# Tail of a hybrid encoder block on one core: order of the last branch blocks, tile pools of the output projection, and the place of loads on the DMA queue

## The chip, the core and the metric

The kernel runs on one core of a Trainium2 chip. A core has five engines with instruction streams of their own: TensorE (PE, matmuls; weight loads are listed apart as PEld), VectorE (DVE), ScalarE (ACT), GpSimd (POOL) and SyncE (SP), which here only issues DMA transfers. Each engine works its stream off in order, and an instruction that waits for a semaphore holds up everything behind it on its engine. SP's stream is the DMA queue of nearly all loads; POOL issues the stores to scratch tensors in device memory and a few loads. The metric is the device time of one execution in microseconds (us), as the median of several runs.

## The reference, cut to what matters

All arrays are float32, with 1024 tokens and width 1024, one layer.

```python
h = rmsnorm(x, norm_g) * (1 + scale) + shift
p = h @ w_in          # q, k, v, z_gla, decay ranks, u, vs, z_gmlp, m_gla, m_gmlp
o = gla(q, k, v, decay)            # both directions, 4 heads, chunks of 64
o = o * rsqrt(mean(o * o) + EPS) * gla_norm_g
y_gla  = (o * silu(z_gla)) @ w_br_gla
y_gmlp = (gelu(u) * spatial_gate(vs) * silu(z_gmlp)) @ w_br_gmlp
merged = sigmoid(m_gla) * y_gla + sigmoid(m_gmlp) * y_gmlp
out = rmsnorm(x + gate * (merged @ w_out), final_g)
```

What follows concerns the last fifth of the kernel: the end of the attention of the last head, the product with `w_br_gmlp` (called yb), the product with `w_br_gla` (ya), the merge, and the product with `w_out` (the projection, o).

## The kernel before, in words

Every float32 operand of a large product is split into a high part (a cast, `S.copy` on ACT to the reduced float32r format) and a low part (the difference, on DVE); each product is three matmuls, high by high, high by low and low by high. `split_w` (L172 to L174) does a split, `stage` (L165) loads 512 KB of weights into a staging tile by a DMA on SP, `fm_weights` (L179) stages and splits the weights of one block of 128 output features, and `tm_weights` (L196) does so for four pieces of a 512-column half of `w_out`, with an optional step on the staged piece in between; for `w_out` that step is `scale_cols` (L1197), which multiplies it by the gate on POOL (L1199).

The program is traced in Python and then ordered by a planner. For each engine it takes the earliest instruction in program order whose inputs, by a timing model, are ready, and lays the streams out that way before the run; tiles are given out in the same pass. `tc.issue_after(ins)` puts what its block traces on the engine of `ins` behind `ins`. Tiles come from pools with a fixed number of buffers: "h" (30 of 128x1024, `ht`), "w" (13 of 128x1024, `w4`), "s" (18 of 128x512, `w2`), and PSUM accumulators "d" (3, `pd`). A DMA into a tile waits until the buffer's last user is done.

**The attention and its filler.** `order` lists 16 units (head, direction and half of the tokens). Between their parts, `dense(n)` (called with `QUOTA`) takes steps of a generator, `filler()` (L1056), which runs a list of jobs: q, k and v products of later heads and then the yb blocks. A job is a pair: what fetches its weights, and what runs it in steps of 12 matmuls (`fm_half`, L965). `filler` fetches the next job's weights after the first step of the job before. yb blocks 0 and 1 run as two jobs, a half of the tokens each, for both blocks (`run_two`); blocks 2 to 7 are one job each, first half, then second half. The evacuation `ev_yb` (L987) loads `tb`, multiplies, and stores to `y2_d`. The input of yb is `GG`, sixteen "h" tiles (high and low of four pieces for each half of the tokens).

`key_ops` (L836) transposes the keys of a unit and casts them (`keh`, L843). The output of a unit is normalised, gated with `z_t` (`zg`) and stored to `g_d`.

**ya.** `GO`, again sixteen "h" tiles, is the gated attention output: for three of four pieces it is loaded back from `g_d` into `gf` (L1126) and split, for the last head it is split from `z_t`. `ya_steps` (L1159, matmuls L1165 to L1167) runs blocks of 128 features: blocks 0 to 2 interleaved, then blocks 3 to 7 one after the other, each with the first half of the tokens and then the second, 24 matmuls a half. `ev_ya` (L1134) loads `ta` and `y2` of its block and half (L1145, L1146), merges on DVE (L1147, L1148) and splits the result into `M` (cast L1149, difference L1150).

**Projection.** `w_o` holds the two 512-column halves of `w_out` (`tm_weights`, L196); the first in "w" tiles, the second in "h" tiles. `dense_o` runs 24 matmuls (`tm_step`, L209 to L211) for each of eight blocks of 128 tokens, with the first three ahead up to their last step. `ev_first` (L1202) loads the residual `res` (L1204, in "h" tiles), adds the accumulator, and multiplies by the final gain `fg` on POOL; `ev_last` adds the second half, normalises and stores.

Of the kernel before, what the change touches and what calls it, by code (L numbers as in the profile page):

```python
# [9 lines left out]
F32 = mybir.dt.float32  # L10
# [7 lines left out]
P = 128  # L18
D = 1024
T = 1024  # L20
KC = D // P
# [10 lines left out]
FB_Q, FB_K, FB_Z, FB_U, FB_ZG, FB_MA, FB_MB, FB_YA, FB_YB = 0, 4, 8, 16, 24, 32, 40, 48, 56  # L32


WVS, WV, WO = 0, 8, 14
# [5 lines left out]
PR_FG, PR_BG, PR_BS, PR_C = 0, 1, 2, 3  # L41
# [3 lines left out]
def hybrid_block_kernel(ctx: ExitStack, tc: tile.TileContext, x, wf, wt, wada, wgate, wvr, wst, alpha, abias,  # L45
                        pcols, prows, out):
    nc = tc.nc
    V, S, G, TE = nc.vector, nc.scalar, nc.gpsimd, nc.tensor
# [20 lines left out]
    y2_d = dram("y2_d", [KC, P, T])  # L69
# [3 lines left out]
    ta_d = dram("ta_d", [KC, P, T])  # L73
# [44 lines left out]
    def ht(shape, dtype, name):  # L118
        return hp.tile(shape, dtype, tag="h", bufs=30, name=nm(name))

    def w4(shape, dtype, name):
        return hp.tile(shape, dtype, tag="w", bufs=13, name=nm(name))
# [38 lines left out]
            H.make(c, half)  # L161

    pin = [True]

    def stage(src):  # L165
        w = w4([P, 1024], F32, "ws")
        i = nc.sync.dma_start(w, src)
        if pin[0]:
            tc.keep_in_program_order(i)
        return w  # L170

    def split_w(w, hi, lo):  # L172
        S.copy(hi, w)  # L173
        V.tensor_tensor(out=lo, in0=w, in1=hi.bitcast(F32), op=ALU.subtract)  # L174

    def flat(t):
        return t.rearrange("p k c -> p (k c)")

    def fm_weights(b):  # L179
        w = stage(wf[b])  # L180
        hi, lo = w4([P, KC, P], F32R, "wh"), w4([P, KC, P], F32R, "wl")
        split_w(w, flat(hi), flat(lo))
        return hi, lo
# [12 lines left out]
    def tm_weights(w0, new, prep=None):  # L196
        pieces = []
        for j in range(4):
            w = stage(wt[w0 + j])
            if prep is not None:  # L200
                prep(w)
            hi, lo = new[j]([P, 2, 512], F32R, "th"), new[j]([P, 2, 512], F32R, "tl")
            split_w(w, flat(hi), flat(lo))
            pieces.append((hi, lo))
        return pieces
# [32 lines left out]
    for b in range(2):  # L238
        pc = pd()
        sl = slice(b * 512, b * 512 + 512)  # L240
# [162 lines left out]
    for a, e in ((0, 3), (3, 6), (6, 8)):  # L403
        n = (e - a) * NV0
        w = w4([P, 1024], F32, "ws")
        nc.sync.dma_start(w[:, 0:n], wvr[:, a * NV0:e * NV0])
        new = w4 if e == KC else ht
        hi, lo = new([P, e - a, NV0], F32R, "tvh"), new([P, e - a, NV0], F32R, "tvl")
# [44 lines left out]
    for b in range(2):  # L453
        pw = pm()
        TE.matmul(pw, lhsT=ones, rhs=wsT[:, 4 * b:4 * b + 4, :].rearrange("p g t -> p (g t)"), start=True, stop=True)
        for i in range(4):
            g = 4 * b + i
# [267 lines left out]
    for c in range(2):  # L725
        hi, lo = H.make(c, 1)
# [109 lines left out]
    def key_ops(un):  # L836
        kh = un["kh"]
        pt = pm()
        for i in range(4):
            TE.transpose(pt[:, i * P:(i + 1) * P], kh[:, i * P:(i + 1) * P], ident)  # L840
        keh = w2([P, 512], F32R, "keh")
        kel = w2([P, 512], F32R, "kel")
        S.copy(keh, pt)  # L843
        V.tensor_tensor(out=kel, in0=pt, in1=keh.bitcast(F32), op=ALU.subtract)
        un.update(keh=keh, kel=kel)

# [25 lines left out]
    units = {}  # L872
# [80 lines left out]
    GG = Act("gg")  # L953
# [33 lines left out]
    def ev_yb(j):  # L987
        def ev(half, acc):
            sl = slice(half * 512, half * 512 + 512)
            t = w2([P, 512], F32, "tb")  # L990
            nc.sync.dma_start(t, tb_d[j, :, sl])
            V.scalar_tensor_tensor(out=t, in0=t, scalar=1.0, in1=acc, op0=ALU.add, op1=ALU.mult)
            G.dma_start(y2_d[j, :, sl], t)
        return ev
# [20 lines left out]
    def run_two(x, evacs):  # L1015

        def run(half):
            def f(ws):
                for w, ev in zip(ws, evacs):
                    yield from fm_half(x, w, half, ev)  # L1020
            return f
        return run
# [3 lines left out]
    held = {}  # L1026

    def hold(name, f):
        def g():
            held[name] = f()  # L1030
            return held[name]
        return g
# [5 lines left out]
    def gg_second():  # L1038
# [3 lines left out]
    jobs = [(lambda: prep_qk(0, True), run_fm(H, ev_k(0))),  # L1042
            (lambda: prep_qk(1, False), run_fm(H, ev_q(1))),
            (lambda: prep_qk(1, True), run_fm(H, ev_k(1))),
            (lambda: v_weights(2, w4), run_v(2)),
            (lambda: prep_qk(2, False), run_fm(H, ev_q(2))),
            (lambda: prep_qk(2, True), run_fm(H, ev_k(2))),
            (lambda: v_weights(3, w4), run_v(3)),
            (hold("qk3", lambda: [prep_qk(3, False), prep_qk(3, True)]), qk3(1)),
            (lambda: held["qk3"], qk3(0)),  # L1050
            (hold("yb", gg_first), yb0(0)),
            (gg_second, yb0(1))]
    for j in range(2, KC):
        jobs.append((lambda j=j: fm_weights(FB_YB + j), run_fm(GG, ev_yb(j), (0, 1))))

    def filler():  # L1056
        ready = jobs[0][0]()
        for n, (_, run) in enumerate(jobs):
            now = ready
            first = True  # L1060
            for _ in run(now):
                if first and n + 1 < len(jobs):
                    ready = jobs[n + 1][0]()
                first = False
                yield

    fill = filler()
# [51 lines left out]
    for half in range(2):  # L1119
        for c in range(KC // 2):  # L1120
            hi, lo = GO.make(c, half)
            sl = slice(half * 512, half * 512 + 512)
            if c < 3:
                g = ht([P, 2, 512], F32, "gf")
                for i in range(2):
                    nc.sync.dma_start(g[:, i, :], g_d[2 * c + i, :, sl])  # L1126
                split_w(flat(g), flat(hi), flat(lo))
            else:
                for i in range(2):
                    split_w(z_t[HEADS - 1][i][:, sl], hi[:, i, :], lo[:, i, :])  # L1130
# [3 lines left out]
    def ev_ya(j, half, acc):  # L1134
        if j < KC - 1:
            if half == 0:
                for n in "hl":
                    M[j, n] = ht([P, T], F32R, "m" + n)
            mh, ml = (M[j, n][:, half * 512:half * 512 + 512] for n in "hl")
        else:  # L1140
            mh, ml = (w2([P, 512], F32R, "m" + n) for n in "hl")
        M[j, half] = mh, ml
        sl = slice(half * 512, half * 512 + 512)
        y2, m = w2([P, 512], F32, "y2"), w2([P, 512], F32, "ta")
        nc.sync.dma_start(m, ta_d[j, :, sl])  # L1145
        nc.sync.dma_start(y2, y2_d[j, :, sl])  # L1146
        V.scalar_tensor_tensor(out=m, in0=m, scalar=1.0, in1=acc, op0=ALU.add, op1=ALU.mult)  # L1147
        V.tensor_tensor(out=m, in0=m, in1=y2, op=ALU.add)  # L1148
        S.copy(mh, m)  # L1149
        V.tensor_tensor(out=ml, in0=m, in1=mh.bitcast(F32), op=ALU.subtract)  # L1150
# [4 lines left out]
        return mh[:, o], ml[:, o]  # L1155

    ya_w, ya_acc = {}, {}

    def ya_steps(j, half, k0, k1):  # L1159
        if k0 == 0:  # L1160
            ya_acc[j, half] = pd()
        acc = ya_acc[j, half]
        hi, lo = ya_w[j]
        for k in range(k0, k1):
            TE.matmul(acc, lhsT=hi[:, k, :], rhs=GO.hi(k, half), start=(k == 0), stop=False)  # L1165
            TE.matmul(acc, lhsT=lo[:, k, :], rhs=GO.hi(k, half), start=False, stop=False)  # L1166
            TE.matmul(acc, lhsT=hi[:, k, :], rhs=GO.lo(k, half), start=False, stop=(k == KC - 1))  # L1167


    for j in range(3):  # L1170
        ya_w[j] = fm_weights(FB_YA + j)
        ya_steps(j, 0, 0, 6)
    for j in range(3):
        ya_steps(j, 0, 6, KC)
        ev_ya(j, 0, ya_acc[j, 0])
    for j in range(3):
        ya_steps(j, 1, 0, KC)
        ev_ya(j, 1, ya_acc[j, 1])
    for j in range(3, KC):
        ya_w[j] = fm_weights(FB_YA + j)  # L1180
        for half in range(2):
            ya_steps(j, half, 0, KC)
            ev_ya(j, half, ya_acc[j, half])


    fg = w4([P, D], F32, "fg")
    G.dma_start(fg, prows[PR_FG].partition_broadcast(P))

    res = [None] * NT
    ev_o = []  # L1190
# [6 lines left out]
    def scale_cols(w, b):  # L1197
        w3 = w.rearrange("p (k c) -> p k c", k=2)
        G.tensor_tensor(out=w3, in0=w3, in1=gate[b].unsqueeze(1).broadcast_to([P, 2, 512]),  # L1199
                        op=ALU.mult)  # L1200

    def ev_first(t, acc):  # L1202
        res[t] = ht([P, D], F32, "res")
        nc.sync.dma_start(res[t], x[t * P:(t + 1) * P, :])  # L1204
        r0 = res[t][:, 0:512]
        ev_o.append(V.tensor_tensor(out=r0, in0=acc, in1=r0, op=ALU.add))
        jk = w2([P, 512], F32, "jk")
        s0 = tiny([P, 1], "o_s0", 2)
        S.activation(jk, r0, AF.Square, accum_out=s0)
        ms[t] = tiny([P, 1], "o_ms", 8)  # L1210
        V.tensor_scalar(ms[t], s0, 1.0 / D, EPS, op0=ALU.mult, op1=ALU.add)
        G.tensor_tensor(out=r0, in0=r0, in1=fg[:, 0:512], op=ALU.mult)
# [39 lines left out]
            o_steps(t, KC - 1 if t in ahead else 0, KC)  # L1252
            evac(t, accs[t])

    w_o = [tm_weights(WO, [w4] * 4, lambda w: scale_cols(w, 0))]
    dense_o(w_o[0], ev_first, range(NT), range(3))
    with tc.issue_after(ev_o[2].ins):
        w_o.append(tm_weights(WO + 4, [ht] * 4, lambda w: scale_cols(w, 1)))
# [79 lines left out]
```

## Time and profile before

| | us |
|---|---|
| median of 3 runs | 1096.53 (1094.05 to 1097.13) |
| the profiled execution | 1096.96 |
| its span | 1095.3 |
| mean granted clock of TensorE | 0.988 of full |
| PE busy, 850 to 900 | 44.22 of 50 |
| PE busy, 950 to 1000 | 38.65 of 50 |
| PE busy, 1000 to 1050 | 50.00 of 50 |
| granted clock, 950 to 1000 | 0.91 |

The profile is one execution, seen by the hardware. "Busy" counts the time in which an engine had an instruction at work; matmuls are pipelined, so a row may show 0.39 us for a matmul while the next starts 0.23 later. "Span" runs from the first to the last instruction; the device time has a little around it. In a row of the timeline stand the start, the length, the engine, the line, the operation and its tiles, how many instructions the row merges, and in brackets the idle time ahead of it and what ended it. In the list of waits stand engine, tile and line, what was waited for, and then the total, the count and the longest. SPq is the queue of SP.

### The profile page before, as it was taken

Reading aid. Unit: us, or ns where it says so; the run is one execution under the profiler, and the core shown is the slowest. Engines: PE = TensorE matmul, PEld = TensorE weight load, DVE = VectorE, ACT = ScalarE, POOL = GpSimd, SP = SyncE. Lnnn points to the kernel's source line nnn. Section 1 sums busy time; section 2 is a strip of 40 time slices with the busy share of each in tenths; the row PEclk is TensorE's granted clock in tenths of the full one; section 3 lists DMA queues with packets and bytes.
Section 4 is the critical chain, followed back from the end, with each engine's and each line's share of the span. In section 5 each row is a group of like instructions: output and inputs, shape, how many; then the busy total and the mean of one; then the engine's idle time right before and its main releaser. Section 6 shows DMA issues by size and latency. Waiting matters only on the chain.

```text
span 1095.3 us, 14011 instructions
## 1 busy us (share of the span) xinstructions
PE 1057.6 (97%) x5292; PEld 892.7 (82%) x5292; DVE 641.1 (59%) x960; ACT 412.1 (38%) x721; POOL 276.1 (25%) x304
## 2 busy tenths in 40 slices
PE   6899999999999999999999999999999989995997
PEld 4688899888888888878888898998888778884886
DVE  5777497346547464664554576658767556345522
ACT  4454334233333323343323546457254253111322
POOL 2311203424334352453402001102011010005510
PEclk9899999999999999999999999999999999997999
DMA  9532276233233323223348024347344385235012
GB/s 362 215 128 70 104 253 221 79 118 104 106 116 106 125 97 119 103 104 135 135 145 291 17 83 149 131 140 250 128 161 136 127 294 183 83 119 193 1 58 96
DMA packets 57032, 152.80 MB, mean 140 GB/s; under 512 B 7457, under 2 KB 15649, under 8 KB 56966
## 3 DMA queue, kind: packets, MB, share of 16 engines
q1 hardware_dynamic: 42198, 102.42, 27.0%
q0 software_dynamic: 14768, 49.50, 12.5%
q8 instruction: 41, 0.67, 0.3%
q14 instruction: 25, 0.20, 0.1%
HBM read 108.90 MB, written 43.00 MB: 139 GB/s over the span
## 4 chain that ended last, share of the span: by engine, by line
PE 81%; DVE 5%; issue 5%; DMA 4%; ACT 2%; POOL 1%; SPq 0%; POOLq 0%; ACTq 0%; DVEq 0%
PE pd L210 5%; PE pd L211 5%; PE po L589 4%; PE po L587 4%; PE po L588 4%; PE pd L209 4%; PE pd L969 4%; PE pd L970 4%; PE pd L971 4%; PE pk L587 3%; PE pk L589 3%; PE pk L588 3%; PE pd L587 3%; PE pd L588 3%; PE pd L589 3%
## 5 line engine op out<-in xcount | busy, mean ns | idle before, releaser
L543 PE MATMUL pd<-tvh,hh 128*128 128x256 f32 (+1 forms) x256 | 75.0, 293 | 0.0
L544 PE MATMUL pd<-tvl,hh 128*128 128x256 f32 (+1 forms) x256 | 73.8, 288 | 0.0
L545 PE MATMUL pd<-tvh,hl 128*128 128x256 f32 (+1 forms) x256 | 73.4, 287 | 0.0
L219 POOL TENSOR_TENSOR r<-ms,nhalf 128x1 f32<-128x1 f32 (+1 forms) x24 | 21.6, 900 | 193.1 <-DVE ms L218 184.5
L589 PE MATMUL pd<-hh,al 128*128 128x512 f32 x160 | 62.5, 390 | 0.0
L587 PE MATMUL pd<-hh,ah 128*128 128x512 f32 x160 | 62.3, 390 | 0.0
L588 PE MATMUL pd<-hl,ah 128*128 128x512 f32 x160 | 62.3, 389 | 0.0
L209 PE MATMUL pd<-th,mh 128*128 128x512 f32 x120 | 47.0, 403 | 7.8 <-ACT th L173 7.8
L969 PE MATMUL pd<-ggh,wh 128*128 128x512 f32 x128 | 51.8, 405 | 1.8 <-ACT wh L173 1.8
L210 PE MATMUL pd<-tl,mh 128*128 128x512 f32 x120 | 48.3, 403 | 3.5 <-DVE tl L174 3.5
L971 PE MATMUL pd<-ggh,wl 128*128 128x512 f32 x128 | 51.6, 405 | 0.0
L970 PE MATMUL pd<-ggl,wh 128*128 128x512 f32 x128 | 51.1, 399 | 0.0
L174 DVE TENSOR_TENSOR al<-wa,ah 128x1024 fp32r<-128x1024 f32 x20 | 31.4, 1571 | 32.7 <-PE po L588 30.8
L1167 PE MATMUL pd<-gl,wh 128*128 128x512 f32 x128 | 49.8, 389 | 0.0
L1166 PE MATMUL pd<-gh,wl 128*128 128x512 f32 x128 | 49.6, 389 | 0.0
L1165 PE MATMUL pd<-gh,wh 128*128 128x512 f32 x128 | 49.6, 389 | 0.0
L610 POOL TENSOR_TENSOR wsum<-wb 128x512 f32<-128x512 f32 x20 | 25.8, 1288 | 94.2 <-DMA wb<-in_wf 69.7
L544 PEld LDWEIGHTS pd<-tvl,hh 128*128 128x128 f32 x256 | 48.7, 190 | 0.9 <-issue 0.5
L543 PEld LDWEIGHTS pd<-tvh,hh 128*128 128x128 f32 x256 | 48.7, 190 | 0.8 <-issue 0.5
L545 PEld LDWEIGHTS pd<-tvh,hl 128*128 128x128 f32 x256 | 48.7, 190 | 0.0
L211 PE MATMUL pd<-th,ml 128*128 128x512 f32 x120 | 48.0, 400 | 0.0
L174 DVE TENSOR_TENSOR wl<-ws,wh 128x1024 fp32r<-128x1024 f32 x24 | 29.3, 1220 | 30.0 <-ACT wh L173 28.8
(318 smaller groups left out, 3108.0 us busy)
## 6 DMA issues: line engine op xcount, KB each, us to landing
ws<-in_wf SPq DMA_DIRECT2D x24, 512.0 KB, 5.3
ws<-in_wt SPq DMA_DIRECT2D x22, 512.0 KB, 4.8
wa<-in_wf SPq DMA_DIRECT2D x20, 512.0 KB, 3.6
wb<-in_wf SPq DMA_DIRECT2D x20, 512.0 KB, 4.6
wa<-in_wada SPq DMA_DIRECT2D x16, 512.0 KB, 9.3
xn<-in_x SPq DMA_DIRECT2D x8, 512.0 KB, 7.4
sg_d<-sg POOLq DMA_DIRECT2D x16, 256.0 KB, 3.1
wg<-in_wgate SPq DMA_DIRECT2D x16, 256.0 KB, 5.3
```

Of the source, the lines that this page charges most:

```text
L209: TE.matmul(acc, lhsT=xh, rhs=hi[:, k % 2, :], start=(k == 0), stop=False)
L210: TE.matmul(acc, lhsT=xh, rhs=lo[:, k % 2, :], start=False, stop=False)
L211: return TE.matmul(acc, lhsT=xl, rhs=hi[:, k % 2, :], start=False, stop=(k == KC - 1))
L543: TE.matmul(acc, lhsT=H.hi_t(k, t), rhs=hi, start=(k == 0), stop=False)
L544: TE.matmul(acc, lhsT=H.hi_t(k, t), rhs=lo, start=False, stop=False)
L545: i = TE.matmul(acc, lhsT=H.lo_t(k, t), rhs=hi, start=False, stop=(k == KC - 1))
L587: TE.matmul(acc, lhsT=a, rhs=xh(k), start=(first and k == 0), stop=False, skip_group_check=not first)
L588: TE.matmul(acc, lhsT=a, rhs=xl(k), start=False, stop=False, skip_group_check=not first)
L589: TE.matmul(acc, lhsT=b, rhs=xh(k), start=False, stop=(k == 3), skip_group_check=not first)
L969: TE.matmul(acc, lhsT=hi, rhs=x.hi(k, half), start=(k == 0), stop=False)
L970: TE.matmul(acc, lhsT=hi, rhs=x.lo(k, half), start=False, stop=False)
L971: TE.matmul(acc, lhsT=lo, rhs=x.hi(k, half), start=False, stop=(k == KC - 1))
```

## The change

yb blocks 6 and 7 become two jobs as blocks 0 and 1 are: both blocks for the first half of the tokens, then both for the second. The filler may fetch two jobs ahead: for the last four jobs the third step also fetches. The splits of `gf` are put behind the cast of the last unit's keys on ACT. ya's block 3 is fetched before the second round of blocks 0 to 2, and each later block a block earlier than it is run; blocks 5 to 7 run the first half of the tokens for all three and then the second. The loads of `ta` and `y2` go behind the latest staged weights on SP, and the loads of the residual behind the last `y2`. `res` moves from "h" to "w" tiles, and the first half of `w_out` from "w" to "h" tiles. The final gain is loaded after the weights' first half is traced.

```diff
     def stage(src):
         w = w4([P, 1024], F32, "ws")
         i = nc.sync.dma_start(w, src)
+        last_w[0] = i
...
-        S.copy(keh, pt)
+        un["ins"] = S.copy(keh, pt)
...
-    for j in range(2, KC):
+    for j in range(2, KC - 2):
         jobs.append((lambda j=j: fm_weights(FB_YB + j), run_fm(GG, ev_yb(j), (0, 1))))
 
+    yb6 = run_two(GG, [ev_yb(j) for j in range(KC - 2, KC)])
+    jobs.append((hold("yb6", lambda: [fm_weights(FB_YB + j) for j in range(KC - 2, KC)]), yb6(0)))
+    jobs.append((lambda: held["yb6"], yb6(1)))
+
     def filler():
-        ready = jobs[0][0]()
+        ready = [jobs[0][0]()]
         for n, (_, run) in enumerate(jobs):
-            now = ready
-            first = True
-            for _ in run(now):
-                if first and n + 1 < len(jobs):
-                    ready = jobs[n + 1][0]()
-                first = False
+            now = ready.pop(0)
+            for part, _ in enumerate(run(now)):
+
+                if part == 0 or part == 2 and n >= len(jobs) - 4:
+                    want = n + 2 + part // 2
+                    for m in range(n + 1 + len(ready), min(want, len(jobs))):
+                        ready.append(jobs[m][0]())
                 yield
...
-                split_w(flat(g), flat(hi), flat(lo))
+                with tc.issue_after(units[order[-1]]["ins"].ins):
+                    split_w(flat(g), flat(hi), flat(lo))
...
-        nc.sync.dma_start(m, ta_d[j, :, sl])
-        nc.sync.dma_start(y2, y2_d[j, :, sl])
+
+        with tc.issue_after(last_w[0].ins):
+            nc.sync.dma_start(m, ta_d[j, :, sl])
+            last_y2[0] = nc.sync.dma_start(y2, y2_d[j, :, sl])
...
+    ya_w[3] = fm_weights(FB_YA + 3)
     for j in range(3):
         ya_steps(j, 0, 6, KC)
         ev_ya(j, 0, ya_acc[j, 0])
     for j in range(3):
         ya_steps(j, 1, 0, KC)
         ev_ya(j, 1, ya_acc[j, 1])
-    for j in range(3, KC):
-        ya_w[j] = fm_weights(FB_YA + j)
+    for j in range(3, 5):
+        ya_w[j + 1] = fm_weights(FB_YA + j + 1)
         for half in range(2):
             ya_steps(j, half, 0, KC)
             ev_ya(j, half, ya_acc[j, half])
 
-
-    fg = w4([P, D], F32, "fg")
-    G.dma_start(fg, prows[PR_FG].partition_broadcast(P))
+    for half in range(2):
+        for j in range(5, KC):
+            if half == 0 and j + 1 < KC:
+                ya_w[j + 1] = fm_weights(FB_YA + j + 1)
+            ya_steps(j, half, 0, KC)
+            ev_ya(j, half, ya_acc[j, half])
+
...
-        res[t] = ht([P, D], F32, "res")
-        nc.sync.dma_start(res[t], x[t * P:(t + 1) * P, :])
+        res[t] = w4([P, D], F32, "res")
+        with tc.issue_after(last_y2[0].ins):
+            nc.sync.dma_start(res[t], x[t * P:(t + 1) * P, :])
...
-    w_o = [tm_weights(WO, [w4] * 4, lambda w: scale_cols(w, 0))]
+    w_o = [tm_weights(WO, [ht] * 4, lambda w: scale_cols(w, 0))]
+    fg = w4([P, D], F32, "fg")
+    G.dma_start(fg, prows[PR_FG].partition_broadcast(P))
     dense_o(w_o[0], ev_first, range(NT), range(3))
```

More of the change, by code (lines that the diff above doesn't have):

```diff
@@ L163, in hybrid_block_kernel @@
     pin = [True]
+    last_w = [None]
     def stage(src):
@@ L1157, in hybrid_block_kernel @@
     ya_w, ya_acc = {}, {}
+    last_y2 = [None]
     def ya_steps(j, half, k0, k1):
```

## The prediction

> **What bounds the kernel now.** I read the page first: which engine is full, and where it is not.
>
> ```profile
> span 1095.3 us, 14011 instructions
> PE 1057.6 (97%) x5292; PEld 892.7 (82%) x5292; DVE 641.1 (59%) x960; ACT 412.1 (38%) x721; POOL 276.1 (25%) x304
> PE   6899999999999999999999999999999989995997
> ```
>
> PE is the bound, and the change neither adds nor removes a matmul. So the time can fall only where PE stands still or runs at a reduced clock. After the start the row of 40 slices is at 9 but for an 8 (slice 33, the last unit of the attention), a 5 (slice 37, the step from the last branch product, ya, L1165, to the output projection, L209) and the end. The waits of PE from 800 us on name them all, and the stage table shows that nothing is to be had between them.
>
> ```profile
> PE pd L209 <- ACT th L173: 7.8, 1, 7.8
> PE pd L210 <- DVE tl L174: 3.5, 1, 3.5
> PE pm L830 <- DVE b L821: 2.6, 1, 2.6
> PE pd L969 <- ACT wh L173: 1.8, 1, 1.8
> PE po L848 <- DVE zg L948: 0.7, 1, 0.7
> PE po L946 <- ACT op L937: 0.5, 1, 0.5
> ...
> 900.00:950.00 50.00, 50.00 (x222) 41.39 (x222) 26.37 (x36) 11.80 (x15) 1.09 (x2) 1.00 0.47 158
> ```
>
> **Step 1, the large gap.** PE's timeline, with start, length and waits, the first three lines from the end of the attention for the pace:
>
> ```profile
> 885.74 0.50 PE L969 MATMUL pd<-ggh,wh 128*128 128x512 f32 x1 [1.83 <-ACT wh L173]
> ...
> 886.31 0.39 PE L969 MATMUL pd<-ggh,wh 128*128 128x512 f32 x1
> 886.54 0.40 PE L970 MATMUL pd<-ggl,wh 128*128 128x512 f32 x1
> ...
> 985.50 0.39 PE L1167 MATMUL pd<-gl,wh 128*128 128x512 f32 x1
> 993.72 1.65 PE L209 MATMUL pd<-th,mh 128*128 128x512 f32 x3 [7.83 <-ACT th L173]
> 998.89 0.80 PE L210 MATMUL pd<-tl,mh 128*128 128x512 f32 x1 [3.52 <-DVE tl L174]
> 999.48 0.63 PE L211 MATMUL pd<-th,ml 128*128 128x512 f32 x1
> ...
> 1004.18 0.51 PE L209 MATMUL pd<-th,mh 128*128 128x512 f32 x1
> 1004.52 0.40 PE L210 MATMUL pd<-tl,mh 128*128 128x512 f32 x1
> ```
>
> At full pace two such matmuls start 0.23 us apart (886.31, 886.54; 0.227 over longer stretches); after the gap they start 0.43 apart (12 of them from 999.48 to 1004.18). From 985.50 to 1004.52 are 19.02 us, in which 17 matmuls start (1, 3, 1 and the 12); at 0.227 they need 3.86. The gap costs **15.2 us**: the waits of 11.3 and 3.9 of cold clock. Its cause stands on SP's queue:
>
> ```profile
> SPq L1204 <- PE pd L1167: 43.7, 4, 41.7
> ...
> 976.18 4.99 SPq L1204 DMA_DIRECT2D res<-in_x  x8
> 981.25 0.51 SPq L1145 DMA_DIRECT2D ta<-ta_d  x1
> ...
> 983.46 23.49 SPq L167 DMA_DIRECT2D ws<-in_wt  x7
> ```
>
> The first residual load stands for 41.7 us at the head of SP's queue, until a ya matmul frees its "h" tile. Behind it are the last merge pair and seven of the eight projection weights. They come at 981 and 983, after eight residual loads, and the first casts and the POOL scalings follow only at 992.6. The change takes this apart in three ways. The residual goes to "w" tiles and behind the last y2 load. Projection halves hi and lo go to "h" tiles, so staging needs 4 "w" tiles and not 12. And the order of blocks 5 to 7 (three first halves, then three second halves) frees the eight first-half tiles of GO while 3 x 24 matmuls x 0.227 = 16.3 us of ya are still to run. In those 16.3 us must happen four casts, four subtractions, and ahead of them the four POOL scalings (the groups by tile, with least, median and longest ns; the landing is that of the staged weights):
>
> ```profile
> L1199 POOL TENSOR_TENSOR ws<-ws,gate x4: 2361/2604/3344, 958.8 to 997.7; 128x1024 f32<-128x1024 f32 x4
> L173 ACT CAST th<-ws x3: 1040/1045/1045, 992.6 to 997.8; 128x1024 fp32r<-128x1024 f32 x3
> L174 DVE TENSOR_TENSOR tl<-ws,th x2: 3360/3370/3380, 995.5 to 998.8; 128x1024 fp32r<-128x1024 f32 x2
> DMA to landing us min/median/max: 3.5/5.9/9.1
> ```
>
> Even one after the other at their worst rows the subtractions take 4 x 3.38 = 13.5, after a cast of 1.04: 14.6, still inside 16.3. The scalings need only staging tiles and the gate rows; the first ran at 958.8 before, 27 us ahead of ya's end, and held nothing up. Three blocks' weights hold 6 of 13 "w" tiles, four staged pieces and the final gain 5: eleven, so they fit. I take the whole 15.2 as gone. What is late next is the first residual, due when three projection tokens have run, 72 matmuls x 0.227 = 16 us after ya; the eight loads took 4.99 us to issue, and a load of the same 512 KB lands in 5.9, at most 9.1. No cost.
>
> **Step 2, the end of the attention.** Two places. The first:
>
> ```profile
> 853.45 0.28 PE L850 MATMUL pk<-vh,kel 128*128 128x256 f32 x1
> 856.33 1.16 PE L830 MATMUL pm<-qh,b 128*128 128x128 f32 x8 [2.60 <-DVE b L821]
> 857.24 0.48 PE L969 MATMUL pd<-ggh,wh 128*128 128x512 f32 x1
> ...
> 861.20 0.39 PE L970 MATMUL pd<-ggl,wh 128*128 128x512 f32 x1
> ...
> 756.85 0.89 PE pm L830 x8
> ```
>
> From 853.45 to 861.20 are 7.75 us; the work in them at full pace is 0.12 for the L850, 0.89 for the eight L830 (the last line, a group that waits for nothing) and ten 512-column matmuls, 2.27: **4.5 us** lost. The chain of work leads back to a load:
>
> ```profile
> 842.50 4.42 DMA gf<-g_d
> ...
> 854.46 1.21 DVE gl L174
> ```
>
> ACT's own timeline, around it and later:
>
> ```profile
> 846.95 1.05 ACT L173 CAST gh<-gf 128x1024 fp32r<-128x1024 f32 x1 [1.32 <-DMA gf<-g_d]
> ...
> 865.14 0.59 ACT L843 CAST keh<-pm 128x512 fp32r<-128x512 f32 x1 [4.33 <-PE pm L840]
> 869.80 0.37 ACT L930 COPY op<-po 128x256 f32<-128x256 f32 x1 [4.07 <-PE po L929]
> ```
>
> ACT stands in order: the cast of GO's third tile waits for its load, and the decay chain (e, L796) waits behind it. The idle time ahead of that cast is 1.32; with its 1.05 that is 2.4, and the subtraction of 1.21 on DVE sits in the same chain: 3.6 us against a wait of 2.6. The change puts the six casts behind the cast of the last unit's keys (865.1), so the chain is free of them. I take 4.5 as gone. The second place is the last unit itself, where fillers are short:
>
> ```profile
> 877.44 7.18 DMA ws<-in_wf
> ```
>
> The weights of yb block 7 are issued at 877.44, because SP's queue holds merge loads ahead of them that wait for "s" tiles and stores. PE waits 1.8 for them, and 0.7 and 0.5 more in steps with nothing to put between. The change fetches blocks 6 and 7 together in the second half of block 4, and holds the merge loads back until ya's fourth weight is issued. That is 20 us and more ahead of the use, against 5.9 to land. These **3.0 us** go too, and since the trace before shows no slow matmuls behind them, nothing more.
>
> [...] The wait of 1.8 was followed by full pace, that of 2.6 by slow matmuls up to 861.20, those of 7.8 and 3.5 by twelve. [...]
>
> **What is added.** The held-back casts: three (3 x 1.05 on ACT, 3 x 1.21 on DVE) now fall in 865 to 873, where ACT idled 4.07 us at a stretch, but where DVE also forms the running state (L867) that PE waits for. At worst each holds a state up by its length: 3.6 us; at best 0, since yb fillers now are there. I take one of three, 1.2. The weights' loads now stand ahead of the merge loads, which landed thus:
>
> ```profile
> DMA to landing us min/median/max: 3.0/3.6/9.3
> ```
>
> The first merge pair is needed 13.6 us after ya begins (60 matmuls), ya's fourth weight is issued by its beginning at the latest, and 5.9 for the weight and 3.6 for a pair fit. I take 0 to 4 for a wait at ya's new order, and 1.5 of it, nearest to the waits of 0.5 to 1.8 that the trace has at such joints. Below nothing none of this can go: in 900 to 950 PE is busy 50.00 of 50 at clock 1.00. Fetching block 5 to 7 by halves adds no instruction.
>
> **Sum.** 15.2 + 4.5 + 3.0 = 22.7 out, 2.7 in: 20.0. The profiled run took 1096.96 for a span of 1095.3, so 1.66 lie around it; its time less 20.0 is 1077.0. The median shown, 1096.53, lies 0.4 below that run. Forecast **1077**; the floor is 1096.96 - 22.7 = 1074.3, and with that 0.4 and the spread of the runs shown (1094.05 to 1097.13) down to 1072.5.
>
> **Rivals.**
> A, only the large gap goes (15.2), and the attention's waits stay or are replaced by others of like size: 1096.96 - 15.2 = 1081.8, with 1 to 2 around it. For it: the order of ACT and DVE there is the planner's, made from estimated times, and before it also put a cast ahead of a late load.
>
> B, the scalings and the merge meet. One merge sum (L1148) that ran beside the first scaling took 2.35 us, the others 0.69:
>
> ```profile
> L1148 DVE TENSOR_TENSOR ta<-ta,y x16: 681/692/2350, 915.4 to 991.4; 128x512 f32<-128x512 f32 x16
> ```
>
> Now all four scalings run beside merges: 4 x 1.66 = 6.6 on the path if it decides, so 1077 + 6.6 = 1083.6; with cold clock after it up to 1086. Against it: with three accumulators each merge has the 24 matmuls of the next half, 5.4 us, as cover. [...]
>
> C, the wait returns under another name: the planner puts a load that waits for a tile ahead of the weights again, and the gap stays: 1094 to 1097.
>
> D, slower: SP's order becomes a chain. Every merge load now stands behind a weight load that waits for a "w" tile. If staged projection weights, the gain and early residuals hold nine or more of 13 tiles, a block's weights can be loaded only when the block before gives up its tiles: 5.9 landing, 1.05 cast, 1.21 subtraction, 8.2 us for each of blocks 3 to 7, 41 in all, less the 22.7: about 1115. It decides from nine tiles on; by my count of program order they hold five until block 7 is staged, since residuals come last.
>
> **How the numbers follow.** Forecast (1073 to 1080) 0.58; A 0.19; B 0.11; C 0.05; D 0.07. The range 1072.5 to 1086 takes in the forecast, A and B and leaves out C and D and some tails. What a measurement of this kernel can tell from no change is about 0.3%, 3.3 us: faster 0.88, the same 0.05, slower 0.07.
>
> **What would show it.** Right: no wait of PE on th or tl at L209 and L210; ya and projection 0.227 apart across the join at clock 1.00; th cast some 10 us before ya's last matmul; residual loads last on SP; the gh casts after the last keh, and no wait at L830; yb 6 and 7 weights landed before the last unit. Wrong: a wait at L1165 for weights or at the accumulators for merge loads, SP standing on L167, or slow matmuls after a new wait.

## The result and the profile after

The changed kernel takes 1079.0 us (median of 4 runs, 1078.18 to 1079.17); the kernel before, with one more run, 1096.83 (1094.05 to 1097.2). The ratio is 0.9841, with a 95% interval from 0.9824 to 0.9858. That is 17.8 us less, where 20 were forecast: inside the range, 2 us above the forecast.

The page of the changed kernel: its span, PE in 40 slices, and the granted clock.

```profile
span 1077.4 us, 14024 instructions
...
PE   6899999999999999999999999999999999998997
...
PEclk9999999999999999999999999999999999999999
```

The 8 at the end of the attention is gone, and the 5 at the join of ya and the projection has become an 8. The waits of PE from 780 us on show what is left:

```profile
PE pd L211 <- ACT th L175: 3.1, 1, 3.1
PE pk L852 <- DVE kel L846: 0.4, 1, 0.4
PE po L948 <- ACT po L933: 0.3, 1, 0.3
PE po L931 <- DVE s L869: 0.2, 1, 0.2
```

(Lines have moved by two in the attention and by eleven in ya's steps: L209 to L211 are now L211 to L213, the splits of L173 and L174 are L175 and L176, ya's matmuls are L1176 to L1178.) The kernel before has two short waits more than the six that the prediction lists: 0.3 for kel at L850 and 0.2 for s at L929. Those two and the 0.5 at L946 are still here, at most 0.4 long, and of the five others only the first survives: the first projection matmul still waits for a cast. PE's timeline there:

```profile
978.08 0.39 PE L1178 MATMUL pd<-gl,wh 128*128 128x512 f32 x1
981.57 1.65 PE L211 MATMUL pd<-th,mh 128*128 128x512 f32 x3 [3.10 <-ACT th L175]
983.02 0.63 PE L212 MATMUL pd<-tl,mh 128*128 128x512 f32 x1
...
984.30 0.50 PE L212 MATMUL pd<-tl,mh 128*128 128x512 f32 x1
984.64 0.39 PE L213 MATMUL pd<-th,ml 128*128 128x512 f32 x1
```

From 978.08 to 984.64 are 6.56 us; eight matmuls start in them (two of the rows between are left out), 1.8 us at full pace. So 4.7 us are still lost of the 15.1 before. SP's queue (start, length, transfers) is what the change made of it: the four staged pieces go at 924 to 935, the merge loads are all out by 938, and the residual waits behind them, where it holds up nothing but the second half of the weights.

```profile
923.87 11.21 SPq L168 DMA_DIRECT2D ws<-in_wt  x4
...
937.80 0.64 SPq L1156 DMA_DIRECT2D y<-y_d  x1
945.63 33.44 SPq L1221 DMA_DIRECT2D res<-in_x  x8
982.80 3.73 SPq L168 DMA_DIRECT2D ws<-in_wt  x4
```

What is late is seen on ACT and POOL. ACT's timeline:

```profile
974.51 0.62 ACT L1159 CAST mh<-ta 128x512 fp32r<-128x512 f32 x1 [4.82 <-DVE ta L1158]
979.95 0.62 ACT L1159 CAST mh<-ta 128x512 fp32r<-128x512 f32 x1 [4.82 <-DVE ta L1158]
980.48 3.88 ACT L175 CAST th<-ws 128x1024 fp32r<-128x1024 f32 x4
```

POOL's:

```profile
947.60 0.54 POOL L1211 DMA_DIRECT2D gate<-gate_d  x1 [11.46 <-DVE ta L1158]
948.95 0.54 POOL L1211 DMA_DIRECT2D gate<-gate_d  x1 [0.82 <-DVE ml L1160]
951.52 10.88 POOL L1215 TENSOR_TENSOR ws<-ws,gate 128x1024 f32<-128x1024 f32 x4 [2.02 <-DMA gate<-gate_d]
```

The pieces are scaled by 962.4, and ACT stood idle for 15.7 of the next 18 us. But the four casts come behind the cast of the very last merge, at 980.48, and ACT started none of them in the idle stretches of 4.15, 4.82 and 4.82 us ahead of the last three merge casts: it took its stream in order.

To compare runs I add up what PE loses from 788 us on, by the rows of its timeline: for each start, the distance to the next less the full pace (0.227 us for 512 columns, 0.115 for 256, 0.111 for 128, as starts lie apart in the traces: in the kernel before 0.12 at 821.04 and 821.16 for 256, and 0.89 for eight of 128), where the excess is over 0.06. "Attention" reaches to 12 us into ya, "join" from the last ya matmul for 24 us. Between the two no run loses more than 0.1.

| kernel | median, us | ratio to before, 95% | attention | join |
|---|---|---|---|---|
| before | 1096.83 | | 16.4 | 15.1 |
| after | 1079.00 | 0.9841 (0.9824 to 0.9858) | 8.7 | 4.7 |
| pools_only | 1087.54 | 0.9921 (0.9904 to 0.9938) | 16.3 | 5.5 |
| residual_queue_only | 1087.10 | 0.9914 (0.9887 to 0.9942) | 12.3 | 7.1 |
| splits_only | 1092.91 | 0.9967 (0.9955 to 0.9978) | 13.3 | 14.8 |
| yb_jobs_only | 1091.99 | 0.9962 (0.9946 to 0.9977) | 12.4 | 15.1 |
| merge_loads_only | 1093.23 | 0.9968 (0.9955 to 0.9981) | 12.9 | 14.3 |
| all_but_splits | 1081.28 | 0.9860 (0.9844 to 0.9875) | 10.2 | 5.4 |
| all_but_yb_jobs | 1080.21 | 0.9852 (0.9832 to 0.9872) | 9.5 | 5.5 |
| all_but_merge_loads | 1080.08 | 0.9850 (0.9828 to 0.9871) | 9.8 | 4.7 |
| old_block_order | 1078.94 | 0.9840 (0.9826 to 0.9855) | 8.0 | 5.2 |
| early_casts | 1072.78 | 0.9788 (0.9774 to 0.9803) | 7.3 | 0.0 |
| gate_rows_early | 1073.48 | 0.9789 (0.9774 to 0.9804) | 8.4 | 0.0 |
| early_casts_old_order | 1073.60 | 0.9792 (0.9773 to 0.9811) | 7.9 | 0.0 |

Lost time fell by 7.7 in the attention and 10.4 at the join, 18.1 together, against 17.9 in the spans (1095.3 to 1077.4). The account closes. The attention column carries noise: up to ya's beginning the changed kernel, old_block_order and early_casts run the same instructions in the same order on PE, ACT and DVE, and their traces give 8.7, 8.0 and 7.3 there.

### The profile page after: what moved, and what is told of

The parts are those of the page before. It is cut to its first block, busy times and chain, and to the rows that moved or that the text cites. A ratio compares the mean times of both kernels' runs of the same rounds, so it can differ in the third digit from the quotient of the medians.

```text
span 1077.4 us, 14024 instructions
## 1 busy us (share of the span) xinstructions
PE 1052.4 (98%) x5292; PEld 889.3 (83%) x5292; DVE 637.9 (59%) x960; ACT 411.2 (38%) x721; POOL 273.5 (25%) x304
## 4 chain that ended last, share of the span: by engine, by line
PE 84%; DVE 6%; ACT 3%; DMA 3%; issue 2%; POOL 2%; POOLq 0%; SPq 0%; ACTq 0%
PE pd L212 4%; PE pd L213 4%; PE pd L211 4%; PE po L590 4%; PE po L589 4%; PE po L591 4%; PE pd L973 4%; PE pd L971 4%; PE pd L972 4%; PE pd L546 3%; PE pd L547 3%; PE pk L589 3%; PE pd L545 3%; PE pd L591 3%; PE pk L591 3%; PE pk L590 3%
## 5 line engine op out<-in xcount | busy, mean ns | idle before, releaser
L176 DVE TENSOR_TENSOR al<-wa,ah 128x1024 fp32r<-128x1024 f32 x20 | 33.0, 1650 | 32.9 <-PE po L590 31.0
L211 PE MATMUL pd<-th,mh 128*128 128x512 f32 x120 | 46.9, 400 | 3.1 <-ACT th L175 3.1
L1176 PE MATMUL pd<-gh,wh 128*128 128x512 f32 x128 | 49.8, 391 | 0.0
L1178 PE MATMUL pd<-gl,wh 128*128 128x512 f32 x128 | 49.8, 389 | 0.0
L213 PE MATMUL pd<-th,ml 128*128 128x512 f32 x120 | 46.9, 392 | 0.0
L971 PE MATMUL pd<-hh,wh 128*128 128x512 f32 x112 | 45.1, 402 | 0.0
```

Of the source, the lines that this page charges most:

```text
L211: TE.matmul(acc, lhsT=xh, rhs=hi[:, k % 2, :], start=(k == 0), stop=False)
L213: return TE.matmul(acc, lhsT=xl, rhs=hi[:, k % 2, :], start=False, stop=(k == KC - 1))
L971: TE.matmul(acc, lhsT=hi, rhs=x.hi(k, half), start=(k == 0), stop=False)
```

## The experiments

The theory once the result was known: the gain is the load that stood at the head of SP's queue, and the casts and weights that came late at the end of the attention; what is left of the gap is the place of four casts on ACT. The rivals were the order of blocks by halves, which my prediction leaned on, and the late arrival of tiles or scaled pieces.

### What is left of the gap

**early_casts.** The gate rows move ahead of the last loop, and the weights are traced inside it:

```diff
     for half in range(2):
         for j in range(5, KC):
             if half == 0 and j + 1 < KC:
                 ya_w[j + 1] = fm_weights(FB_YA + j + 1)
+            if half == 1 and j == 7:
+                w_o.append(tm_weights(WO, [ht] * 4, lambda w: scale_cols(w, 0)))
             ya_steps(j, half, 0, KC)
```

> The changed kernel, with the first half of the projection's weights (and the gate rows that scale them) traced ahead of the second half of block 7, so that the four casts th stand before the last merge casts on ACT. Theory: what is left of the gap (978.08 to 984.64 in the changed kernel's trace, 6.56 us for 8 matmuls of 0.227, so 4.7 us lost) comes from the place of these casts alone, behind the cast of the last merge; then no wait at the first projection matmul, clock 1.00 across the join, and 1079.0 - 4.7 = 1074.3. Rival: the casts are late because their tiles or the scaled pieces are; then the wait stays at some 3 us, or comes back as a wait of ya on its accumulators, and the time stays at 1078 to 1080.

1072.78 us, and no wait at the join. Its ACT timeline:

```profile
955.96 0.62 ACT L1159 CAST mh<-ta 128x512 fp32r<-128x512 f32 x1 [4.82 <-DVE ta L1158]
956.49 2.98 ACT L175 CAST th<-ws 128x1024 fp32r<-128x1024 f32 x3
959.77 1.06 ACT L175 CAST th<-ws 128x1024 fp32r<-128x1024 f32 x1 [0.31 <-PE pd L1177]
```

The fourth cast waits for a ya matmul: that is the tile of GO that the first halves free. The last ya matmul starts at 975.85, the first of the projection 0.23 later, at 976.08. The theory holds for the gap (0 instead of 4.7). The median fell by 6.2, which is 1.5 more than the gap; the profile has 1.4 of it in the attention, where both kernels run the same instructions in the same order, so I count it as variation between runs.

**gate_rows_early.** Why did the planner put the casts last? Here only the gate's two loads move:

```diff
+    gate = [w2([P, 512], F32, "gate") for _ in range(2)]
+    for b in range(2):
+        G.dma_start(gate[b], gate_d[b].partition_broadcast(P))
     GO = Act("g")
```

> The changed kernel with only the two loads of the gate rows traced ahead of the branch product ya instead of behind it; the projection's weights stay where they are in the program. In the changed kernel the gate rows are loaded at 947.6 and 949.0, after waiting for s tiles that the merge loads hold, and the four scalings run from 951.5 to 962.4. Theory: the planner put the casts last because the scalings come late, and these because of the gate rows; then the casts stand early and the rest of the gap (4.7 us) goes, 1072 to 1075, as with the weights traced earlier. Rival: the place of the weights in the program is what counts; the casts stay last and the time at 1078 to 1080.

1073.48 us. POOL's timeline shows the gate rows loaded at 860 and 871 and the scalings 23.5 us earlier than in the changed kernel; on ACT the casts moved with them, with the weights left where they stood in the program:

```profile
927.99 8.04 POOL L1215 TENSOR_TENSOR ws<-ws,gate 128x1024 f32<-128x1024 f32 x3 [34.87 <-DMA ws<-in_wt]
937.67 2.55 POOL L1215 TENSOR_TENSOR ws<-ws,gate 128x1024 f32<-128x1024 f32 x1 [1.08 <-DMA ws<-in_wt]
```

```profile
958.03 2.98 ACT L175 CAST th<-ws 128x1024 fp32r<-128x1024 f32 x3
961.31 1.06 ACT L175 CAST th<-ws 128x1024 fp32r<-128x1024 f32 x1 [0.30 <-PE pd L1181]
```

So the chain of the remaining gap is: gate rows wait for "s" tiles that merge loads hold, hence the scalings are late, hence the planner put the casts behind the last merge; and there ACT ran them, at 980.48, though the pieces were ready at 962.4, 18 us before. That moving the two loads moves the casts is shown; that it goes through the planner's estimated times is inferred from how the planner works, for no run shows the estimates themselves. This version is the fastest but for early_casts, from which its interval does not set it apart: 22.9 us below the kernel before (1096.42 when measured beside it) and 5.5 below the changed one, with two loads moved.

**old_block_order.** The changed kernel, blocks 5 to 7 run as before:

```diff
-    for half in range(2):
-        for j in range(5, KC):
-            if half == 0 and j + 1 < KC:
-                ya_w[j + 1] = fm_weights(FB_YA + j + 1)
+    for j in range(5, KC):
+        if j + 1 < KC:
+            ya_w[j + 1] = fm_weights(FB_YA + j + 1)
+        for half in range(2):
             ya_steps(j, half, 0, KC)
             ev_ya(j, half, ya_acc[j, half])
```

> The changed kernel with blocks 5 to 7 of the branch product in the order of before (both halves of a block one after the other). My prediction's step: the order by halves frees tiles 16.3 us before the end and so carries the gain; without it the tiles come free only in the last 5.4 us and the gap grows by 3 to 6 us, to 1082 to 1085. Rival: in the changed kernel the casts stand behind the last merge cast anyway, so the early tiles are not used: gap 4.7 as now, 1079 within 1.

1078.94, the same. The wait of 3.1 at L211 is the same too. In the changed kernel the tiles that the order by halves frees early are not used early.

**early_casts_old_order.** The early casts with that old order:

> The kernel with the early casts, but blocks 5 to 7 in the order of before. Now the casts could use the tiles that the order by halves frees early. Theory: with casts early the order matters a little; the tiles come free 5.4 us before the end, four casts and subtractions need 1.04 + 4 x 1.22 = 5.9, and the first matmuls need only the first pieces: 0 to 1.5 us more than the early casts, 1073 to 1075. Rival (my prediction's step): without the 16.3 us the conversions do not fit and 3 us or more of the gap return, 1076 to 1079.

1073.60 against 1072.78, with intervals that overlap, and no wait at the join. Here the casts run from 967.87 to 973.0, between merge casts, and that is early enough for a projection that begins at 977.38. So the order by halves buys nothing that a run here can measure, even where its tiles are used.

### The large gap

**pools_only** and **residual_queue_only** take the kernel before. The first swaps the pools, queues the residual, and loads the final gain after the weights (the last is left out here):

```diff
-        res[t] = ht([P, D], F32, "res")
-        nc.sync.dma_start(res[t], x[t * P:(t + 1) * P, :])
+        res[t] = w4([P, D], F32, "res")
+        with tc.issue_after(last_y2[0].ins):
+            nc.sync.dma_start(res[t], x[t * P:(t + 1) * P, :])
...
-    w_o = [tm_weights(WO, [w4] * 4, lambda w: scale_cols(w, 0))]
+    w_o = [tm_weights(WO, [ht] * 4, lambda w: scale_cols(w, 0))]
```

> The kernel before, with only the tile pools swapped (residual in w tiles, first half of the projection's weights in h tiles, gain loaded later) and the residual's loads behind the last y2 load. Theory: the residual load at the head of SP's queue is the cause of the large gap; alone this takes the gap from 15.2 to about 4.7 us, 1096.8 - 10.5 = 1086.3, and leaves the waits at the end of the attention (2.6 and 1.8). Rival: without the new block order and the new place of the merge loads the queue blocks elsewhere, and the gap stays above 10: 1092 to 1097.

The second has only the `issue_after`, with `res` in "h" tiles:

> The kernel before, with only the residual's loads put behind the last y2 load on SP; all tiles stay in their pools. Theory: the load at the head of the queue alone makes the large gap; the gap shrinks from 15.1 to some 5 us as with the pools swapped, 1086 to 1089. Rival: the tiles count too: the projection's weights then need 12 of 13 w tiles, of which ya's blocks hold 4, and half of the gap stays, 1090 to 1094.

1087.54 and 1087.10. The first lands 1.2 above its theory. Its waits, from 780 us on:

```profile
PE pd L209 <- ACT th L173: 3.1, 1, 3.1
PE pm L830 <- DVE b L821: 3.0, 1, 3.0
PE pd L969 <- ACT wh L173: 1.1, 1, 1.1
```

The join is nearly that of the changed kernel (5.5 against 4.7), the attention that of the kernel before (16.3 against 16.4): the swap and the queue act on the join alone. The second kernel is told by its SP and PE timelines:

```profile
971.24 5.20 SPq L1206 DMA_DIRECT2D res<-in_x  x8
976.49 23.08 SPq L167 DMA_DIRECT2D ws<-in_wt  x7
```

```profile
984.06 0.97 PE L209 MATMUL pd<-th,mh 128*128 128x512 f32 x3 [3.10 <-ACT th L173]
985.32 0.57 PE L210 MATMUL pd<-tl,mh 128*128 128x512 f32 x1 [0.29 <-DVE tl L174]
...
992.57 0.50 PE L210 MATMUL pd<-tl,mh 128*128 128x512 f32 x1 [1.25 <-DVE tl L174]
```

The residual still stands ahead of seven weights, but no longer ahead of the last merge pair, and that alone brings the first wait from 7.8 to 3.1: in the kernel before, the cast th waited on ACT behind a merge whose `ta` came at 990.66, as its DVE and ACT timelines have it:

```profile
990.66 0.69 DVE L1147 SCALAR_TENSOR_TENSOR ta<-ta,pd 128x512 f32<-128x512 f32 x1 [7.37 <-DMA ta<-ta_d]
992.10 0.62 ACT L1149 CAST mh<-ta 128x512 fp32r<-128x512 f32 x1 [9.54 <-DVE ta L1148]
992.63 1.04 ACT L173 CAST th<-ws 128x1024 fp32r<-128x1024 f32 x1
```

In residual_queue_only the same cast runs at 982.96, right behind the last merge cast at 982.44. The late weights then cost a second wait of 1.25 and a join of 7.1 rather than 5.5. So what the residual held up that mattered most was the last merge load. The runs of this kernel spread from 1083.96 to 1090.67, and its profile is of the fastest, so its 12.3 in the attention is not to be read as an effect of the edit. By the medians (1087.54 and 1087.10) the swap of pools adds nothing to the queue's part that these runs can show, except that the four times of pools_only lie within 0.3 of each other; the swap without the queue was not run.

### The end of the attention

**splits_only**, the kernel before with `tc.issue_after(units[order[-1]]["ins"].ins)` around the splits of `gf`:

> The kernel before, with only the splits of gf put behind the cast of the last unit's keys. Theory: the 2.6 us wait at L830 and the slow matmuls behind it go, 4.5 us: 1096.8 - 4.5 = 1092.3; the later waits (1.8, 0.7, 0.5, and 7.8 and 3.5) stay. Rival: the casts are moved into the last unit, where ACT and DVE also make its states, and the wait comes back there: 1095 to 1098.

1092.91, 3.6 less. The wait at L830 is gone from the list; the last unit now waits 0.8 for its weights and 0.8 in all for states, near the 1.2 that I had set for the moved casts. The profiled run is the slowest of six and has a stretch at clock 0.50 from 878.3 to 881.7, though no wait near it is longer than 0.8 (see the last section).

**yb_jobs_only**, the kernel before with the new jobs and `filler`:

> The kernel before, with only yb blocks 6 and 7 by halves and the filler's deeper prefetch. Theory: the weights of block 7 are late because they are fetched late; fetched with block 6 two jobs earlier they land before the last unit, and its 3.0 us of waits plus about 1 us of small pauses go: 1096.8 - 4 = 1092.8. Rival: they are late because merge loads stand ahead of them on SP; then the weights still land at about 884 and the waits stay: 1095 to 1098.

**merge_loads_only**, the kernel before with the merge loads behind the staged weights:

> The kernel before, with only the merge loads put behind the latest staged weights on SP. Theory (fetch order in the program is what counts): the weights of yb block 7 come a little earlier, 0 to 2 us won, the large gap stays, 1095 to 1097. Rival (the queue is what counts): with the merge loads out of the way the weights of block 7 land before the last unit, its 3.0 us of waits and 1 us of pauses go: 1092.8.

1091.99 and 1093.23. Each alone removes the wait for block 7's weights, so the theory of the second expectation falls and its rival stands beside the first: fetch order and queue are two cures for one wait. In yb_jobs_only the weights go out at 819.74, in the kernel with the merge loads held back at 864, 13 us earlier than before. SP's timelines, of the one and the other:

```profile
819.74 0.33 SPq L167 DMA_DIRECT2D ws<-in_wf  x1
```

```profile
841.95 22.23 SPq L993 DMA_DIRECT2D tb<-tb_d  x7
864.22 0.90 SPq L168 DMA_DIRECT2D ws<-in_wf  x2
```

Left out of the changed kernel one at a time:

> The changed kernel with the yb jobs of before (blocks 6 and 7 one after the other, one job of prefetch). Theory: the late weights return and with them 3 to 4 us: 1082 to 1083. Rival: with the merge loads held back the queue is free and the weights come in time without it: 1079 within 1.

> The changed kernel with the merge loads free to be issued as early as before. Theory: the early prefetch of the yb weights is enough; 1079 within 1.5. Rival: merge loads clog the queue at the end of the attention again; 1082 to 1084.

> The changed kernel with the splits of gf free on ACT as before. Theory: the wait of 2.6 us at the decay chain returns with its slow matmuls, 3.5 to 4.5 us: 1082.5 to 1083.5. Rival: with the other edits the loads of gf land earlier or PE has filler at that place, and little returns: 1079 to 1080.

1080.21, 1080.08 and 1081.28: 1.2, 1.1 and 2.3 more than the changed kernel. The first two differences lie within the intervals and within the noise of the attention, so no cost is shown for leaving out either; that either cure does without the other is shown by the waits, where block 7's weights cost 0.5 in all_but_yb_jobs and nothing in all_but_merge_loads. Alone the four parts bring, each against the kernel before as measured beside it (1096.5 and 1096.55), 9.0 (pools), 3.6 (splits), 4.6 (yb jobs) and 3.3 (merge loads), 20.5 in all, against 17.8 for the whole; the overlap fits yb jobs and merge loads, which cure one wait. The first of the three misses its theory (1082 to 1083), and its rival (1079 within 1) by 0.2. The last misses both (1082.5 to 1083.5, 1079 to 1080): its wait of 2.4 at the decay chain returns, but not the slow matmuls that I had priced with it (below).

## Why the prediction was right, and where it was not

**The large gap.** The mechanism was right: the load at the head of SP's queue. The size was not: "I take the whole 15.2 as gone", and 10.4 went. The step that failed is "the scalings need only staging tiles and the gate rows; the first ran at 958.8 before, 27 us ahead of ya's end, and held nothing up". I worked out that scalings and casts fit into the last 16.3 us of ya, and in early_casts they do; I did not ask where the planner would set the casts in ACT's stream. It set them behind the last merge cast, because of the late gate rows, and early_casts and gate_rows_early show 0.0 for the join once they stand earlier. The term left over is 4.7 (3.26 beyond the pace ahead of the first matmul, 1.48 behind it, where matmuls start 0.43 apart and the granted clock is 0.50 from 981.11 to 984.52); I had 1.5 for "a wait at ya's new order", in another place. So two of my signs of being right did not come: PE still waits on th, and the casts th start 2.4 us after ya's last matmul and not some 10 before it.

**The order by halves.** I made it the source of the 16.3 us in which the conversions fit. The runs show it is not needed: 1078.94 without it, 1073.60 with early casts and without it.

**The end of the attention.** I had 4.5 and 3.0 out and 1.2 in, 6.3; the lost time fell by 7.7, which the noise of that column does not set apart from 6.3 or 7.5. Both waits are gone in the changed kernel. L832 (the former L830) runs without one, and the first of the moved casts sits right behind the keys, as ACT's timeline of the changed kernel has it:

```profile
860.72 0.59 ACT L845 CAST keh<-pm 128x512 fp32r<-128x512 f32 x1 [2.52 <-PE pm L842]
861.20 1.06 ACT L175 CAST gh<-gf 128x1024 fp32r<-128x1024 f32 x1
```

The 1.2 for moved casts was not paid: the waits of 0.4, 0.3 and 0.2 are what the attention has left. Where the yb jobs are those of before, in splits_only and all_but_yb_jobs, PE waits 0.8 for states in the last unit, so it is the fillers that cover the casts, as my "at best 0" had it. The rest of the 8.7 is mostly pauses of some 0.1 to 0.2 us at changes from one chain to the next; they stand in both kernels (864.86 to 865.17 before, 876.37 to 876.79 after, where 0.23 is the pace) and make little of the difference.

**The sum.** 22.7 out became 18.1 (7.7 and 10.4), and of the 2.7 in next to nothing came; the two errors partly cancel, 20.0 against 17.9 in the spans, so that the time came within 2 us of the forecast is in part luck.

**The rivals.** A and C are excluded by the list of waits. D too: PE does not wait once in ya. B I can read directly, since the four scalings ran beside merges. DVE's timeline of the changed kernel:

```profile
952.03 2.44 DVE L1158 TENSOR_TENSOR ta<-ta,y 128x512 f32<-128x512 f32 x1
955.16 2.14 DVE L1160 TENSOR_TENSOR ml<-ta,mh 128x512 fp32r<-128x512 f32 x1 [0.69 <-ACT mh L1159]
957.22 0.67 DVE L1157 SCALAR_TENSOR_TENSOR ta<-ta,pd 128x512 f32<-128x512 f32 x1
957.93 2.19 DVE L1158 TENSOR_TENSOR ta<-ta,y 128x512 f32<-128x512 f32 x1
960.81 2.13 DVE L1160 TENSOR_TENSOR ml<-ta,mh 128x512 fp32r<-128x512 f32 x1 [0.69 <-ACT mh L1159]
```

The four operations with two operands in SBUF (952.03, 955.16, 957.93, 960.81) take 2.1 to 2.4 us beside the scalings and 0.69 elsewhere; the one that reads the accumulator in PSUM, at 957.22, keeps its 0.67. PE does not feel it: it does not wait once in ya, where the 24 matmuls of a half take 5.4 us (24 x 0.227).

## What to carry to other kernels

When a wait at the head of a DMA queue is taken away, follow the freed data one stage further, to the place of its first consumer in that engine's stream: a planner can leave a cast last in line although its input has been ready for 18 us. Look for what its order hung on; here it was two small loads that waited for a tile. And where two edits aim at one wait, try each alone before both are kept: either of two removed the late weights, and the new block order did nothing that a run here can tell from noise.

## What the runs showed of the hardware that was not expected

In these runs the price of a short wait of PE is not a function of its length. The wait at the decay chain stands in several kernels. In all_but_splits it is 2.37 us, the next 512-column matmuls start some 0.24 apart, and the granted clock stays at 1.00; in merge_loads_only it is 2.19, they start 0.43 apart, and the clock falls to 0.50. Over 14 us around this wait the mean granted clock is 0.88 with waits of 2.19 (merge_loads_only), 2.60 (before), 2.71 (yb_jobs_only) and 3.02 (pools_only), and 1.00 with 2.01 (residual_queue_only) and 2.37.

The traces say more on this than the lengths do. In the kernel before, from 800 us to 1007.82, the granted clock is 0.50 from 857.64 to 861.05 and from 990.76 to 1004.41, which is 3.41 and 13.65 us, with 129.71 at 1.00 between; 13.65 and 129.71 are 4 and 38 times 3.41. In the changed kernel it is 0.50 from 981.11 to 984.52, again 3.41, and 1.00 from 800 us up to there. Here are the two waits with stretches of that length, set whole times 3.41 us from where the clock of their trace changes (PE busy is the first number behind the comma, the clock the third from the end), first all_but_splits:

```profile
841.96 1.16 PE L832 MATMUL pm<-qh,b 128*128 128x128 f32 x8 [2.37 <-DVE b L823]
...
840.18:843.59 3.41, 1.63 (x11) 1.54 (x12) 3.41 (x7) 0.00 (x0) 0.54 (x1) 1.00 0.49 153
843.59:847.01 3.42, 3.42 (x16) 2.80 (x16) 2.72 (x5) 2.14 (x3) 0.54 (x1) 1.00 0.66 238
```

The same of merge_loads_only:

```profile
855.55 1.73 PE L832 MATMUL pm<-qh,b 128*128 128x128 f32 x8 [2.19 <-DVE b L823]
...
852.56:855.97 3.41, 1.22 (x8) 0.93 (x8) 3.41 (x5) 0.89 (x2) 0.00 (x0) 1.00 0.00 0
855.97:859.38 3.41, 3.41 (x13) 2.93 (x12) 3.17 (x7) 0.00 (x0) 1.07 (x2) 0.50 0.41 154
```

The shorter wait falls whole into one stretch, which has 2.2 us without a matmul, and the next stretch runs at 0.50; the longer one is cut in two, 0.6 and 1.8, and nothing follows. The kernel before has 2.1 us without a matmul from 854.23 to 857.64, ahead of its 0.50, and 1.2 from 878.12 to 881.53, followed by 1.00. In splits_only 1.2 us, the longest wait 0.73, were followed by 0.50, with eight 128-column matmuls against the identity between the waits:

```profile
874.90:878.32 3.42, 2.18 (x11) 1.22 (x11) 1.74 (x4) 1.72 (x5) 0.46 (x1) 1.00 1.03 372
878.32:881.73 3.41, 3.40 (x11) 3.04 (x12) 1.97 (x3) 1.23 (x2) 0.00 (x0) 0.50 1.04 399
```

So in these traces idle time alone does not decide, and what else counts stays open. From the two waits shown I estimate that one of just over 2 us costs its own length or, with the clock at 0.50 for 3.41 us, up to 1.7 us more (half of 3.41). The traces show that the stretch ahead of one at 0.50 need not be idle throughout; no run moved a wait against these stretches on purpose.
